# One more of eight u/gate pairs computed with seven block products: NF from 3 to 2 in a hybrid diffusion step

## The chip, the cores and the metric

The kernel runs on one core of a Trainium2 chip. The metric is the time of one execution on the device, in microseconds (us). Engines: PE multiplies matrices, DVE and ACT work element by element, POOL (GpSimd) does a few sums, SP issues the DMAs. Each engine works through its own list of instructions in order.

## The reference, cut to what matters

```
proj = jnp.matmul(h, p['w_in'])                  # h: 640 tokens x 2048
q, k, v, g_a, xbc, z, dt_raw, u, v_c, g_c, g_m = jnp.split(proj, _in_splits(), -1)
...
# branch C, the spatial gating unit
vs = jnp.einsum('gpq,bcqge->bcpge', p['w_s'], vn) + ...
y = u.astype(f32) * vs.reshape(b_, L, SGU_W) * jax.nn.silu(gate.astype(f32))   # gate is g_c
```

One input projection feeds three branches. Its columns are cut into tiles of 128 channels. Of u there are eight tiles, and eight of the gate g_c; u tile g and gate tile g are needed together with vs tile g. The 640 tokens are those of the prompt (128) and of the sample (512) together.

## The kernel before, in words

All large products are done in float32r with each operand split in two: hi is the value rounded to float32r, lo is what is left. A product is hi by hi, hi by lo, lo by hi: three matmuls.

**A plain tile** (`plain`, L207) multiplies one weight tile (16 blocks of 128 rows) with the 640 tokens in two halves of 320 columns: 16 x 3 x 2 = 96 matmuls of 320 columns. Its weights come in two DMAs (L125) of 1024 columns, ACT makes `whi` (L135) and DVE `wlo` (L136), 512 columns (four blocks) at a time.

**A pair** (`pair`, L219) computes two weight tiles at once. The two tiles, the two halves of the 2048 inner rows and the two halves of the tokens make a 2 by 2 block product, which is done with seven products instead of eight, by sums of blocks on both sides: 7 x 8 x 3 = 168 matmuls of 320 columns. The seven products are numbered 1 to 7. The weights' side is made in `fetch`: four DMAs (L184), the sums on POOL (L190, L191, L192, L198), then `parts`: ACT `whi` (L166) and DVE `wlo` (L167), in the order p1, p6, p7, p5, p4, p2, p3, two pieces of 512 columns each. The rings hold five raw weight buffers (`wraw`), four pieces of `whi` and of `wlo` (two products), and two sums (`s`).

The tokens' side of the pairs is made once, for k = 0 to 7: `make_t(k)` loads h again from DRAM (`ta`, `tb`, or `u`/`c` for the even k; L607 to L614), makes four differences on DVE (L617 to L620, 320 columns each) and splits three of them into `t12` (used by products 6 and 5) and `t4` (product 4) with `split_to` (ACT L597, DVE L598). The fourth difference, t3, later overwrites the second half of h_hi[k] and h_lo[k] (`make_t3`, names `hh` and `hl`), which a plain tile still reads; product 7 reads it. `ta` and `tb` of odd k have one buffer each, so a load for k + 2 waits until k is done.

The order of the program: after the normalisation stages one plain tile (NT_C), then the plain tiles of the first NF u/gate pairs, with the calls of `make_t` spread between them, then the `make_t3`, then the remaining u/gate pairs by seven products, then 51 more pairs of other columns, then the branches' projections with the attention between them, then the output projection.

```
    wseq = [("plain", NT_C)] + [("plain", n + g) for g in range(NF) for n in (NT_U, NT_GC)]
    wseq += [("pair", NT_U + g, NT_GC + g) for g in range(NF, 8)]
    ...
    fill = [(n + g, g) for g in range(NF) for n in (NT_U, NT_GC)]
    ...
        for k in range(i * 8 // len(fill), (i + 1) * 8 // len(fill)):
            make_t(k)
    for k in range(8):
        make_t3(k)
```

After each u/gate pair `post_c` (L550) multiplies: SiLU of the gate (ACT L546, DVE L547), u times vs (DVE L554), and the product of both on POOL (L555). The order on each engine is made by the scheduler of the language when the program is built, so a change of NF can move instructions that the source does not touch.

Of the kernel before, what the change touches and what calls it, by code (L numbers as in the profile page):

```python
# [19 lines left out]
EPS = 1e-6  # L20
NEG = -1.0e30
HALF = 320
NF = 3
MG = (6, 8, 10, 12)
SCRATCH = 1024

# [8 lines left out]
def hybrid_step(ctx: ExitStack, tc: tile.TileContext, a: dict, o: dict):  # L35
# [105 lines left out]

    wseq = [("plain", NT_C)] + [("plain", n + g) for g in range(NF) for n in (NT_U, NT_GC)]
    wseq += [("pair", NT_U + g, NT_GC + g) for g in range(NF, 8)]
    gates = [("pair", NT_GM + 16 * b + d, NT_GM + 16 * b + d + 1) for b in (2, 1, 0) for d in range(0, KD, 2)]
# [74 lines left out]
    def pair(job, B, tmp, out, seven=(1, 6, 7, 5, 4, 2, 3), side={}):  # L219

        ws = take(*job)
        ac = two_banks()
        bank = {1: ac[0], 5: ac[1], 6: sm_tile(), 7: sm_tile(), 4: sm_tile()}
        bank[2], bank[3] = bank[1], bank[5]
        t1, u2, u3 = (tmp(i) for i in range(3))
        c12, c21, c22 = out()
        done = set()
        for i in seven:  # L230
            ps = bank[i][:, :HALF]
            n = len(ws[i])
            for k, ((wh, wl), (bh, bl)) in enumerate(zip(ws[i], B[i])):
                TE.matmul(ps, wh, bh, start=(k == 0 and i not in (2, 3)), stop=False, skip_group_check=True)  # L234
                TE.matmul(ps, wh, bl, start=False, stop=False, skip_group_check=True)  # L235
                mm = TE.matmul(ps, wl, bh, start=False, stop=(k == n - 1), skip_group_check=True)  # L236
            done.add(i)
            at = None
            if i == 1:
                at = S.copy(t1, ps)  # L240
            if i == 6:
                at = V.tensor_tensor(u2, bank[6][:, :HALF], t1, op=ALU.add)
            if i in (6, 7) and {6, 7} <= done:
                at = V.tensor_tensor(u3, bank[7][:, :HALF], u2, op=ALU.add)
            if i in (7, 5) and {6, 7, 5} <= done:
                at = V.tensor_tensor(c22, bank[5][:, :HALF], u3, op=ALU.add)
            if i in (7, 4) and {6, 7, 4} <= done:
                at = V.tensor_tensor(c21, u3, bank[4][:, :HALF], op=ALU.subtract)
            if i == 3:
                at = V.tensor_tensor(c12, bank[5][:, :HALF], u2, op=ALU.add)  # L250
            for work in side.get(i, ()):
                work(mm, at)
        return [bank[1][:, :HALF], c12], [c21, c22]
# [265 lines left out]
    def post_conv(t, x):  # L519

        xq = pad[-1]
        S.copy(xq[:, 1:129], x[0][:, 0:128])
        S.copy(xq[:, 131:323], x[0][:, 128:320])
        S.copy(xq[:, 323:643], x[1])
        y = cvp.tile([P, 642], F32, tag="cvy", name="cvy")
        cw = cwh[:, 16 + 3 * t:16 + 3 * t + 3]
        V.tensor_scalar(y, xq[:, 1:643], cw[:, 1:2], cwh[:, t:t + 1], op0=ALU.mult, op1=ALU.add)
        V.scalar_tensor_tensor(out=y, in0=xq[:, 0:642], scalar=cw[:, 0:1], in1=y, op0=ALU.mult, op1=ALU.add)
        V.scalar_tensor_tensor(out=y, in0=xq[:, 2:644], scalar=cw[:, 2:3], in1=y, op0=ALU.mult, op1=ALU.add)
        r = gp.tile([P, 642], F32, tag="raw", name="cv")  # L530
        S.activation(r, y, AF.Tanh)
        V.scalar_tensor_tensor(out=r, in0=r, scalar=1.0, in1=y, op0=ALU.add, op1=ALU.mult)
        nc.sync.dma_start(out=cv_dram[:, t, :P], in_=r[:, :P])
        store(cv_dram[:, t, P:], r[:, 130:642])
# [15 lines left out]
    def post_c(g, u, gc):  # L550
        t = load_raw(g)
        for h in range(2):
            hs = (H1, H2)[h]
            V.tensor_tensor(t[:, hs], t[:, hs], u[h], op=ALU.mult)  # L554
        G.tensor_tensor(t, t, silu_of(gc), op=ALU.mult)  # L555
        nc.sync.dma_start(out=o_dram["c"][:, g, :], in_=t)
# [85 lines left out]
    post_conv(12, [b[:, :HALF] for b in ac])  # L642
    fill = [(n + g, g) for g in range(NF) for n in (NT_U, NT_GC)]
    u = None
# [25 lines left out]

    for g in range(NF, 8):
        x, y = pair(("pair", NT_U + g, NT_GC + g), HB, tmp_g, out_g,
                    (1, 2, 6, 5, 4, 7, 3) if g == NF else (1, 6, 7, 5, 4, 2, 3))
        post_c(g, x, y)
# [746 lines left out]
```

## Time and profile before

| what | value |
|---|---|
| median of 3 runs | 2521.35 us (2520.49 to 2522.02) |
| the profiled execution's own time | 2522.39 us |
| its span, first to last instruction | 2520.6 us |
| PE busy | 2429.2 us, 96% |
| DVE busy | 1735.2 us, 69% |
| ACT busy | 1084.2 us, 43% |
| POOL busy | 801.2 us, 32% |
| mean granted PE clock | 0.993 |

The span is what the profile's rows can explain; the 1.8 us around it are the start and the end of the execution. The shares are means over stages with different limits. The stretch that the change touches lies between about 270 and 400 us.

### The profile page before, as it was taken

What the parts mean: (1) busy time and instruction counts of PE and PEld (TensorE: products, weight loads), DVE (VectorE), ACT (ScalarE), POOL (GpSimd) and SP (SyncE); (2) the same over time, 40 slices, a digit from 0 to 9 for tenths busy, and PEclk for the clock granted to TensorE, in tenths of its full rate; (3) what the DMA queues carried; (4) which work ended last, traced back from release to release, by engine and by line L of the source; (5) the groups of instructions that cost most, each with busy time, mean ns of one, the idle gap of its engine ahead of it and who ended that gap; (6) DMA issues with size and microseconds to landing.
All of it is one profiled execution on the core that took longest, in us unless ns stands there. A gap on an engine that the chain in (4) does not pass through costs nothing. (4 is left out here: it accounts for less than half of the span.)

```text
span 2520.6 us, 43220 instructions
## 1 busy us (share of the span) xinstructions
PE 2429.2 (96%) x16615; PEld 2298.4 (91%) x16615; DVE 1735.2 (69%) x2788; ACT 1084.2 (43%) x2340; POOL 801.2 (32%) x369
## 2 busy tenths in 40 slices
PE   6989999999999999999999999999999999999998
PEld 4679999999999999999999999989998888998886
DVE  5454688888888778767677767777545555537975
ACT  4122233444444555565555554554323666322222
POOL 2100045444444344434333344344232233331001
PEclk9999999999999999999999999999999999999999
DMA  9953433333333444443444444434987554545544
GB/s 374 340 180 109 159 117 111 105 115 116 109 106 115 140 140 134 163 156 127 151 140 134 138 128 158 142 121 155 332 308 258 170 182 133 155 122 195 178 141 166
DMA packets 154072, 411.13 MB, mean 163 GB/s; under 512 B 16965, under 2 KB 29546, under 8 KB 153866
## 3 DMA queue, kind: packets, MB, share of 16 engines
q1 hardware_dynamic: 151562, 407.33, 48.4%
q8 instruction: 130, 2.13, 0.3%
q10 hardware_dynamic: 2304, 1.05, 0.1%
q14 instruction: 76, 0.62, 0.1%
HBM read 333.50 MB, written 74.81 MB: 162 GB/s over the span
## 5 line engine op out<-in xcount | busy, mean ns | idle before, releaser
L167 DVE TENSOR_TENSOR wlo<-wraw,whi 128x512 fp32r<-128x512 f32 x448 | 612.0, 1383 | 127.6 <-ACT whi L166 121.6
L166 ACT CAST whi<-wraw 128x512 fp32r<-128x512 f32 x448 | 275.1, 617 | 312.7 <-PE acca L235 147.4
L135 ACT CAST whi<-wraw 128x512 fp32r<-128x512 f32 (+1 forms) x238 | 140.3, 593 | 413.8 <-PE bk L824 140.5
L236 PE MATMUL acca<-hh,wlo 128*128 128x320 f32 x896 | 280.5, 313 | 15.0 <-DVE wlo L167 14.9
L166 ACT CAST whi<-s 128x512 fp32r<-128x512 f32 x336 | 203.0, 617 | 206.5 <-PE sm L235 82.5
L167 DVE TENSOR_TENSOR wlo<-s,whi 128x512 fp32r<-128x512 f32 x336 | 232.7, 693 | 73.6 <-ACT whi L166 69.5
L234 PE MATMUL acca<-hh,whi 128*128 128x320 f32 x896 | 278.5, 311 | 1.4 <-ACT whi L166 1.4
L235 PE MATMUL acca<-hl,whi 128*128 128x320 f32 x896 | 277.5, 310 | 0.0
L190 POOL TENSOR_TENSOR s<-wraw 128x1024 f32<-128x1024 f32 x56 | 145.7, 2602 | 369.3 <-DMA wraw<-in_w_nt 243.3
L136 DVE TENSOR_TENSOR wlo<-wraw,whi 128x512 fp32r<-128x512 f32 (+1 forms) x218 | 155.5, 716 | 143.7 <-ACT whi L135 143.0
L191 POOL TENSOR_TENSOR s<-s,wraw 128x1024 f32<-128x1024 f32 x56 | 150.3, 2684 | 261.0 <-DVE wlo L167 260.9
L198 POOL TENSOR_TENSOR s<-wraw,s 128x1024 f32<-128x1024 f32 x56 | 138.6, 2475 | 209.7 <-issue 189.5
L236 PEld LDWEIGHTS acca<-hh,wlo 128*128 128x128 f32 x896 | 168.7, 188 | 21.4 <-DVE wlo L167 21.1
L234 PEld LDWEIGHTS acca<-hh,whi 128*128 128x128 f32 x896 | 169.1, 189 | 2.0 <-ACT whi L166 2.0
L235 PEld LDWEIGHTS acca<-hl,whi 128*128 128x128 f32 x896 | 169.0, 189 | 0.0
L824 PE MATMUL bk<-oh,whi 128*128 128x320 f32 x512 | 163.6, 319 | 2.2 <-ACT oh L1014 1.5
L824 PE MATMUL bk<-ol,whi 128*128 128x320 f32 x512 | 158.5, 310 | 1.0 <-DVE ol L1015 0.5
L824 PE MATMUL bk<-oh,wlo 128*128 128x320 f32 x512 | 158.3, 309 | 0.0
L236 PE MATMUL sm<-t4h,wlo 128*128 128x320 f32 x448 | 142.5, 318 | 14.2 <-DVE wlo L167 14.2
L192 POOL TENSOR_TENSOR wraw<-wraw 128x1024 f32<-128x1024 f32 x56 | 152.1, 2715 | 4.3
L234 PE MATMUL sm<-t4h,whi 128*128 128x320 f32 x448 | 140.5, 314 | 1.9 <-ACT whi L166 1.9
L235 PE MATMUL sm<-t4l,whi 128*128 128x320 f32 x448 | 140.3, 313 | 0.0
(406 smaller groups left out, 6961.5 us busy)
## 6 DMA issues: line engine op xcount, KB each, us to landing
wraw<-in_w_nt SPq DMA_DIRECT2D x240, 512.0 KB, 3.8
wm<-in_w_ms SPq DMA_DIRECT2D x64, 512.0 KB, 7.4
wraw<-in_w_br SPq DMA_DIRECT2D x48, 512.0 KB, 4.8
wm<-in_w_mg SPq DMA_DIRECT2D x32, 512.0 KB, 3.9
wraw<-in_w_out SPq DMA_DIRECT2D x31, 512.0 KB, 3.9
g_gate<-sg SPq DMA_DIRECT2D x48, 320.0 KB, 2.6
gt<-g_gate SPq DMA_DIRECT2D x48, 320.0 KB, 4.4
ac_d<-Y SPq DMA_DIRECT2D x32, 256.0 KB, 3.1
```

The source lines that it names most:

```text
L135: S.copy(hi[:, :n], rv)
L136: eng.tensor_tensor(lo[:, :n], rv, hi[:, :n].bitcast(F32), op=ALU.subtract)
L166: S.copy(hi, src[:, i:i + 512])
L167: V.tensor_sub(lo, src[:, i:i + 512], hi.bitcast(F32))
L190: G.tensor_tensor(s1, a21, a22, op=ALU.add)
L191: G.tensor_tensor(s2, s1, a11, op=ALU.subtract)
L192: G.tensor_tensor(a21, a11, a21, op=ALU.subtract)
L198: G.tensor_tensor(s2, a12, s2, op=ALU.subtract)
L234: TE.matmul(ps, wh, bh, start=(k == 0 and i not in (2, 3)), stop=False, skip_group_check=True)
L235: TE.matmul(ps, wh, bl, start=False, stop=False, skip_group_check=True)
L236: mm = TE.matmul(ps, wl, bh, start=False, stop=(k == n - 1), skip_group_check=True)
L824: newest[0] = TE.matmul(*args, **kw)
```

## The change

One number changes: NF, the count of u/gate pairs whose two tiles are computed plainly.

```
-NF = 3
+NF = 2
```

Pair 2 (u tile 2 and gate tile 2) leaves the plain tiles and becomes the first of now six u/gate pairs by seven products. It takes the order (1, 2, 6, 5, 4, 7, 3) in the source that pair 3 had. The list `fill` has four plain tiles instead of six, so two `make_t` fall to each, where before it was one or two.

The built programs differ between the first plain tiles and the second pair, and again in some forty rows at the start of the attention, where branch B's operands are made (L1014, L1015); elsewhere the rows are the same.

On POOL, the three sums of the first pair's weights (s1, s2 and the difference in wraw) stand here before the change, behind both products of the first two gated tiles (L555):

```order
L555 TENSOR_TENSOR raw_2875<-raw_2875,sg_2879 128x640
L555 TENSOR_TENSOR raw_3167<-raw_3167,sg_3171 128x640
L190 TENSOR_TENSOR s1_3337<-wraw_3331,wraw_3333 128x1024
L191 TENSOR_TENSOR s2_3338<-s1_3337,wraw_3329 128x1024
L192 TENSOR_TENSOR wraw_3331<-wraw_3329,wraw_3331 128x1024
L198 TENSOR_TENSOR s2_3338<-wraw_3335,s2_3338 128x1024
```

and with the change:

```order
L555 TENSOR_TENSOR raw_2889<-raw_2889,sg_2893 128x640
L190 TENSOR_TENSOR s1_3090<-wraw_3084,wraw_3086 128x1024
L191 TENSOR_TENSOR s2_3091<-s1_3090,wraw_3082 128x1024
L192 TENSOR_TENSOR wraw_3084<-wraw_3082,wraw_3084 128x1024
L198 TENSOR_TENSOR s2_3091<-wraw_3088,s2_3091 128x1024
L555 TENSOR_TENSOR raw_3248<-raw_3248,sg_3252 128x640
L190 TENSOR_TENSOR s1_3316<-wraw_3310,wraw_3312 128x1024
L192 TENSOR_TENSOR wraw_3310<-wraw_3308,wraw_3310 128x1024
```

The first pair's sums moved ahead of the second L555, and the second pair's sums follow right behind it.

On DVE, from the first difference of k = 5 (L617, which needs the load `tb`) the rows before the change are these; `wlo` of L136 belongs to a plain tile:

```order
L617 TENSOR_TENSOR t3c_3184<-tb_3314,ta_3313 128x320
L618 TENSOR_TENSOR ta_3313<-ta_3313 128x320
L617 TENSOR_TENSOR t3d_3512<-c1_3509,ta_3506 128x320
L619 TENSOR_TENSOR tb_3314<-tb_3314,ta_3313 128x320
L136 TENSOR_TENSOR wlo_3068<-wraw_3061,whi_3067 128x512
L618 TENSOR_TENSOR ta_3506<-ta_3506 128x320
```

and with the change, down to the first weights of product 7 (`wlo_3112`):

```order
L617 TENSOR_TENSOR t3c_3055<-tb_3067,ta_3066 128x320
L167 TENSOR_TENSOR wlo_3108<-s2_3091,whi_3107 128x512
L547 SCALAR_TENSOR_TENSOR sg_3252<-sg_3252,acca_3080 128x320
L618 TENSOR_TENSOR ta_3066<-ta_3066 128x320
L547 SCALAR_TENSOR_TENSOR sg_3252<-sg_3252,accb_3081 128x320
L598 TENSOR_TENSOR t4l2_2458<-u0_3051,t4h2_2457 128x320
L598 TENSOR_TENSOR hl5_841<-t3c_3055,hh5_126 128x320
L617 TENSOR_TENSOR t3d_3265<-c1_3262,ta_3259 128x320
L167 TENSOR_TENSOR wlo_3112<-wraw_3084,whi_3111 128x512
```

Pieces of the first pair's weights (`wlo_3108` is the second half of product 6, `wlo_3112` the first half of product 7) and the `make_t3` splits (`hl5`) now stand among the differences.

On PE, the first pair comes to product 7 in this order with the change (`sm2` collects product 6, `sm3` product 7):

```order
L235 MATMUL sm2_3380<-t12l4_2446,whi_3107 128x320
L236 MATMUL sm2_3380<-t12h4_2445,wlo_3108 128x320
L234 MATMUL sm3_3381<-hh0_121,whi_3111 128x320
L235 MATMUL sm3_3381<-hl0_547,whi_3111 128x320
L236 MATMUL sm3_3381<-hh0_121,wlo_3112 128x320
```

The last of these is the 42nd matmul of that pair; before the change two more plain tiles stood in this place.

## Rows read from the trace of the kernel before

**Rows 1.** The page: PE's busy time, share of the span and instructions.
```profile
PE 2429.2 (96%) x16615; PEld 2298.4 (91%) x16615; DVE 1735.2 (69%) x2788; ACT 1084.2 (43%) x2340; POOL 801.2 (32%) x369
```

**Rows 2.** Windows: from:to, length, busy us (instructions) by engine, PE clock, DMA.
```profile
324.60:341.90 17.30, 15.18 (x98) 14.12 (x97) 16.04 (x27) 7.32 (x18) 4.30 (x2) 1.00 0.36 115
341.90:371.85 29.95, 28.58 (x194) 28.16 (x193) 23.93 (x28) 11.88 (x22) 13.87 (x6) 1.00 0.35 112
371.85:396.50 24.65, 24.65 (x171) 24.65 (x170) 20.93 (x26) 9.53 (x16) 12.34 (x6) 1.00 0.34 113
```

**Rows 3.** Timeline of PE: start, duration, instruction, [idle before <-releaser].
```profile
310.55 0.31 PE L217 MATMUL acca<-hh,whi 128*128 128x320 f32 x1
...
326.70 0.41 PE L217 MATMUL acca<-hh,wlo 128*128 128x320 f32 x1 [1.31 <-DVE wlo L136]
...
365.00 0.41 PE L236 MATMUL acca<-hh,wlo 128*128 128x320 f32 x1 [1.37 <-DVE wlo L167]
...
371.85 0.31 PE L234 MATMUL sm<-t12h,whi 128*128 128x320 f32 x1
```

**Rows 4.** Timeline of DVE, the same columns.
```profile
307.36 0.68 DVE L136 TENSOR_TENSOR wlo<-wraw,whi 128x512 fp32r<-128x512 f32 x1
307.96 0.48 DVE L598 TENSOR_TENSOR t12l<-tb,t12h 128x320 fp32r<-128x320 f32 x1
308.36 0.48 DVE L618 TENSOR_TENSOR ta<-ta 128x320 f32<-128x320 f32 x1
308.76 0.48 DVE L598 TENSOR_TENSOR t4l<-tb,t4h 128x320 fp32r<-128x320 f32 x1
...
314.61 0.49 DVE L617 TENSOR_TENSOR t3c<-tb,ta 128x320 f32<-128x320 f32 x1 [2.75 <-DMA tb<-h_d]
...
321.15 2.70 DVE L598 TENSOR_TENSOR t12l<-ta,t12h 128x320 fp32r<-128x320 f32 x1
...
375.57 0.49 DVE L242 TENSOR_TENSOR u<-sm,u 128x320 f32<-128x320 f32 x1 [0.56 <-PE sm L236]
```

**Rows 5.** Timeline of POOL, the same columns.
```profile
320.91 2.59 POOL L190 TENSOR_TENSOR s<-wraw 128x1024 f32<-128x1024 f32 x1 [0.84 <-DMA wraw<-in_w_nt]
...
326.05 2.85 POOL L192 TENSOR_TENSOR wraw<-wraw 128x1024 f32<-128x1024 f32 x1
343.98 2.42 POOL L198 TENSOR_TENSOR s<-wraw,s 128x1024 f32<-128x1024 f32 x1 [15.07 <-DVE wlo L167]
...
374.36 2.09 POOL L555 TENSOR_TENSOR raw<-raw,sg 128x640 f32<-128x640 f32 x1 [2.02 <-DVE raw L554]
```

**Rows 6.** Timeline of SP's DMA issues.
```profile
270.30 12.05 SPq L125 DMA_DIRECT2D wraw<-in_w_nt  x3
...
309.27 0.32 SPq L608 DMA_DIRECT2D tb<-h_d  x1
```

**Rows 7.** The page, DMA issues: count, KB each, us from issue to landing.
```profile
wraw<-in_w_nt SPq DMA_DIRECT2D x240, 512.0 KB, 3.8
```

**Rows 8.** Tile tb, 290 to 340 us (three loads).
```profile
DMA to landing us min/median/max: 2.9/4.9/5.2
```

**Rows 9.** Waits of PE, 1930 to 1980 us: total, times, longest.
```profile
PE sm L827 <- DVE mx L1039: 1.7, 1, 1.7
PE bk L824 <- ACT oh L1014: 1.5, 1, 1.5
```

**Rows 10.** Timeline of PE at 37 us.
```profile
37.23 0.50 PE L331 MATMUL v<-whi,hh 128*128 128x512 f32 x1 [2.49 <-ACT hh L359]
```

**Rows 11.** Windows of PE alone: from:to, length, busy (instructions), granted clock, DMA.
```profile
38.00:39.00 1.00, 1.00 (x4) 0.65 1.02 410
39.00:40.00 1.00, 1.00 (x4) 0.50 1.02 406
40.00:41.00 1.00, 1.00 (x4) 0.50 1.03 410
41.00:42.00 1.00, 1.00 (x4) 0.64 1.06 422
```

## The prediction

> **What bounds the kernel now.** I read the page first: PE is busy for 96% of the span [rows 1], so a change pays only by taking matmuls away or waits before them. The windows then show that the stretch around the change is not yet at that bound. The window 371.85:396.50 is one whole pair in its steady state: 24.65 us for 168 matmuls, with PE busy throughout, so 0.1467 us each [rows 2]. The two windows before it hold 2.1 and 1.4 us in which PE is idle outright, and more in which it only refills [rows 2].
>
> I take as the measuring stretch everything from the start of plain tile u2, at 310.55 us, to product 6 of pair 4, at 371.85 us [rows 3]: 61.30 us. It holds two plain tiles (192 matmuls), pair 3 (168) and product 1 of pair 4 (24), 384 in all: 384 x 0.1467 = 56.3 us. The other 5.0 us are waits. The timeline of PE shows the two largest: 1.31 us for the wlo of a plain tile and 1.37 us for the wlo of a pair [rows 3]. DVE was late because POOL was adding. L190 to L192 run from 320.91 to 328.90 us, and the DVE split that starts at 321.15 us takes 2.70 us in place of 0.48 us: it ends at 323.85 us, 0.34 us after L190's end at 323.51 [rows 4, 5]. A DVE instruction with one operand in PSUM keeps its 0.49 us while L555 runs [rows 4, 5]. So each POOL sum holds up one DVE instruction that reads only SBUF until the sum is over.
>
> **What the change takes away.** Pair 2 needs 168 matmuls instead of 192: 24 x 0.1467 = 3.5 us. The same stretch after the change holds 360 matmuls, 52.8 us, so without any wait it would end 8.5 us earlier: 3.5 us of matmuls and the 5.0 us of waits. The break-even is therefore 8.5 us of waits after the change, and the question is how many there will be.
>
> **What it adds beside PE.** ACT gets 6 more casts, DVE 6 more wlo at 0.60 us and five combinations at 0.40 us, their pitches in the timeline [rows 4], POOL four more sums of 2.4 to 2.9 us [rows 5]. In 25 us per pair these fit: the steady pair shows DVE busy 20.9 of 24.65 us, POOL 12.3 and ACT 9.5 with no wait [rows 2]. The four weight DMAs are those of the plain tiles, under another line. I cost these at nothing there. Around the first pair there is no such cover, because DVE must also make the operands.
>
> **The first pair's sums.** Its third weight block takes the place of the last of the three DMAs that run from 270.30 to 282.35 us, so it lands by about 282.0 + 3.8 = 285.8 us [rows 6, 7]. L190 to L192 then take 8.0 us [rows 5] and end near 293.8 us, before the differences begin. That removes the collision of 320.91 to 328.90 us.
>
> **The operands.** The plain tiles end at 310.55 instead of 341.9 us. The load of tb for k = 5 waits until the last split of k = 3 has freed the buffer. Before, that split starts at 308.76 and the load is issued at 309.27 us [rows 4, 6]. After the change two more DVE instructions (the splits of make_t3 and one difference that moved behind) stand ahead of it, 2 x 0.40 us, so the load is issued near 310.1 and lands, 4.9 to 5.2 us later [rows 8], near 315.2 us. Before, this wait (2.75 us, to 314.61 [rows 4]) hurt nobody, since the pair began 27 us later. Now the first pair is already running, and DVE's queue stands behind that load.
>
> **Wait A.** PE starts the pair at 310.55 and needs the first wlo of product 7 as its 42nd matmul: 310.55 + 41 x 0.1467 = 316.6 us. On DVE eight instructions from the late difference on stand ahead of that wlo: seven at 0.40 and one at 0.60, 3.4 us, then 0.68 for itself: 315.2 + 3.4 + 0.7 = 319.3 us. The wait is at least 2.7 us. But POOL's L198 can start as soon as product 6's wlo is done, at 316.3, and holds the next difference until 0.34 us past its end: 316.3 + 2.4 + 0.3 = 319.1 us. Then come SiLU, one split, and L555, which starts behind the SiLU near 319.5 us, runs 2.1 us and holds the split hl5 to 321.9 us. L617 and the wlo follow: 322.9 us. Wait A is 6.3 us by this, and I take it, since the trace has the same collision at full price.
>
> **Wait B.** From 322.9 us PE has 48 matmuls (7.0 us) to the first wlo of product 4, so it would be there at 329.9 us. Pair 3's third weight block can be fetched when product 7's second wlo is done, at 324.3; it lands near 328.3 us with 3.8 us of DMA [rows 7], and L190 and L192 run from 328.3 to about 333.6 us. They catch a t12 split of k = 6, which then ends at 331.1, and the wlo of product 4, which ends at 334.0 us. PE waits 1.4 and 2.7 us. The operands of k = 7 come last on DVE, each 0.4 us before its matmul; small waits of 1.3 us in all. Wait B is 5.4 us. Without a collision those for k = 7 come to 4.3 us instead, because tb of k = 7 is then what is late; that is its lower end.
>
> **The sum.** 6.3 + 5.4 = 11.7 us of waits against the 8.5 us of the break-even: +3.2 us. From pair 3 on the rows are the old ones. The lower bound is 2.7 + 4.3 = 7.0, that is -1.5 us. The upper one adds to both waits a load that is 1 us later, and a pair 3 that starts with its weights late: about +6. The profiled execution took 2522.39 us (span 2520.6), 1.0 above the median; the difference applies to both, and on the median of 2521.35 I forecast **2524.5 us**. The permuted rows at the attention's start I cost at nothing: the waits near them are 1.7 and 1.5 us [rows 9], so I allow 2 us on either side.
>
> **The rivals.** A measurement of this kernel tells a change from none at about 0.2%, 5.0 us.
>
> *Faster: the operands come in time.* If DVE catches up because neither L198, L555 nor the next L190 hits it and both tb loads land in 2.9 us as the fastest did [rows 8], the waits come to about 3 us and the time to 2516 us; with none, 2512.9. It decides if wait A and B together stay under 3.5 us. Against it stands the queue: even free of POOL the wlo is ready 2.7 us late.
>
> *No collision, but the late loads.* The lower bound above: 2519.9 us. It asks that POOL's sums fall between DVE's instructions. Against it: L198 is released by the very wlo that the next difference follows on DVE, so the two meet.
>
> *Slower by over 0.2%: PE's clock falls.* At 37 us, after 2.49 us idle, the granted clock goes to half, 1.2 GHz: four slices of 1 us show 0.65, 0.50, 0.50, 0.64 [rows 10, 11], a loss of 0.35 + 0.5 + 0.5 + 0.36 = 1.7 us. Wait A is longer than that idle time, and so a fall behind it is likely. It costs nothing as long as PE only comes later to wait B, which has 5.4 us to absorb 1.7. A second fall behind wait B has only the small waits of k = 7 to hide in. With one fall in the open +4.9, with both +6.6: 2526.2 to 2528 us. It decides where wait B ends later on PE's side than on DVE's.
>
> The Trainium skill, "TensorE: Matmul & The Clock Gate", Part 1, says that the throttled clock is the default and activity releases it, so a wait in mid-kernel is paid twice. By that rule both falls would be paid and the sum would be +6.6; by this case's rows the first hides in a wait that DVE sets, and the sum stays at +3.2. The trace agrees that idle time halves the clock (0.50 after 2.49 us), but shows no fall with DVE-bound work behind it.
>
> **Chances.** Forecast (waits of 10 to 13 us): 0.52, of which 0.08 lies beyond +5. No collision: 0.18. Faster: 0.07. Clock or a later stall that spreads to pair 3: 0.23, nearly all beyond +5. Hence faster 0.07, within 0.2% 0.63, slower 0.30. The range for 8 in 10 reaches from the lower bound less 1 us to two clock falls: 2518.9 to 2528.5 us.
>
> **What would show it.** In the profile after the change: 24 fewer matmuls; L190 to L192 of the first pair near 286 to 294 us; DVE idle for tb until about 315 us; a PE wait of about 6 us for wlo of L167 near 317 us and two more near 330; DVE instructions of 2 to 3 us under L198, L555, L190; product 6 of pair 4 near 374.5 instead of 371.85 us. The prediction is wrong if PE's waits between 310 and 345 us stay under 7 us, if the clock stays at half past 340 us, or if later pairs start to wait.

## The result and the profile after

The changed kernel takes 2536.44 us (median of 4 runs, 2533.68 to 2541.16) where the kernel before takes 2520.92 us on the same chip: a ratio of 1.0058, 95% interval [1.0043, 1.0073]. It is 15.5 us slower; the forecast was +3.2 us. The profiled execution took 2541.16 us (span 2539.4 us), 18.8 us over that of before.

The page of the changed kernel has the 24 matmuls less, and its instruction fetches are two rows of the DMA queues (packets, MB, share of 16 engines):

```profile
PE 2435.5 (96%) x16591; PEld 2301.5 (91%) x16591; DVE 1741.0 (69%) x2799; ACT 1088.7 (43%) x2347; POOL 811.9 (32%) x373
...
q8 instruction: 130, 2.13, 0.4%
...
q14 instruction: 77, 0.63, 0.1%
```

The timeline of PE around the first pair, to be held against [rows 3]:

```profile
317.14 0.41 PE L236 MATMUL sm<-t12h,wlo 128*128 128x320 f32 x1 [1.88 <-DVE wlo L167]
...
323.53 0.63 PE L236 MATMUL sm<-hh,wlo 128*128 128x320 f32 x1 [5.07 <-DVE wlo L167]
323.96 0.47 PE L234 MATMUL sm<-hh,whi 128*128 128x320 f32 x1
324.23 0.47 PE L235 MATMUL sm<-hl,whi 128*128 128x320 f32 x1
...
336.30 0.42 PE L234 MATMUL sm<-hh,whi 128*128 128x320 f32 x1 [1.76 <-ACT hh L597]
...
376.99 0.31 PE L234 MATMUL sm<-t12h,whi 128*128 128x320 f32 x1
```

The first pair starts at 309.53 us here, and product 6 of pair 4 at 376.99: 67.46 us, against 61.30 us in the same stretch of before. Here the change costs 6.2 us. Of the 67.46 us, 52.8 are matmuls at full clock and 8.7 are the three waits; the other 6.0 us are the clock and the refilling behind waits. Behind the wait of 5.07 us the matmuls follow each other by 0.27 us in place of 0.1467 us: TensorE runs at the lower of its two levels, 1.2 GHz. The clock had fallen before that wait, behind the first one of 1.88 us: in windows of 1 us it is 0.77 from 317 us, 0.50 in each window from 318 to 327, and 1.00 from 328 us. It falls again behind the wait of 1.76 us: 0.51, 0.50 and 0.50 from 338 to 341 us. The windows of the changed kernel (PE, PEld, DVE, ACT, POOL, granted clock, DMA) show the same in steps of 10 us:

```profile
310.00:320.00 10.00, 6.58 (x39) 5.69 (x38) 7.65 (x14) 4.17 (x11) 2.36 (x1) 0.88 0.52 174
320.00:330.00 10.00, 6.47 (x31) 6.47 (x32) 9.70 (x19) 4.60 (x10) 1.91 (x2) 0.61 0.41 126
330.00:340.00 10.00, 7.95 (x43) 6.57 (x42) 8.89 (x12) 4.22 (x9) 4.93 (x2) 0.90 0.16 60
340.00:350.00 10.00, 10.00 (x65) 10.00 (x65) 9.10 (x16) 4.47 (x8) 2.69 (x1) 0.93 0.33 110
350.00:360.00 10.00, 10.00 (x71) 10.00 (x70) 8.41 (x10) 3.99 (x7) 4.53 (x2) 1.00 0.42 128
```

The timelines of DVE and POOL show the load of tb and the collisions, as [rows 4, 5] did for before:

```profile
316.00 0.49 DVE L617 TENSOR_TENSOR t3c<-tb,ta 128x320 f32<-128x320 f32 x1 [2.35 <-DMA tb<-h_d]
...
317.40 2.52 DVE L618 TENSOR_TENSOR ta<-ta 128x320 f32<-128x320 f32 x1
...
320.65 1.82 DVE L598 TENSOR_TENSOR hl<-t3c,hh 128x320 fp32r<-128x320 f32 x1
```

```profile
285.97 2.40 POOL L190 TENSOR_TENSOR s<-wraw 128x1024 f32<-128x1024 f32 x1 [2.58 <-DMA wraw<-in_w_nt]
...
317.22 2.36 POOL L198 TENSOR_TENSOR s<-wraw,s 128x1024 f32<-128x1024 f32 x1 [23.56 <-DVE wlo L167]
320.40 1.72 POOL L555 TENSOR_TENSOR raw<-raw,sg 128x640 f32<-128x640 f32 x1 [0.82 <-DVE sg L547]
```

So far this is close to what the prediction drew. But the stretch explains only 6.2 of the 15.5 us. Laid over each other pair by pair (start of product 1 to start of the next), the two traces agree within 0.01 us from pair 5 to 640 us, 24.64 to 25.73 us each; then the changed kernel loses at some pairs and gains at others (the pair at 1253 us in before takes 28.28 us there, 25.08 us after). The largest loss in a pair is at the one that starts at 871.5 us in before: 24.64 us there, 28.85 us after. These are its start and the next one's, first before, then after:

```profile
871.49 0.31 PE L234 MATMUL acca<-hh,whi 128*128 128x320 f32 x1
...
896.13 0.31 PE L234 MATMUL acca<-hh,whi 128*128 128x320 f32 x1
```

```profile
876.98 0.31 PE L234 MATMUL acca<-hh,whi 128*128 128x320 f32 x1
...
905.83 0.31 PE L234 MATMUL acca<-hh,whi 128*128 128x320 f32 x1
```

The chain behind the loss is short. xk_d, ac_d and cv_d are scratch tensors in DRAM through which another branch passes its data while the pairs run. In the timelines of SP, ACT and PE of the changed kernel, two stores go out at 884.28 and 884.75 us; the load behind them (L689) reuses the first one's buffer and is issued only when that store has landed; ACT's casts stand behind its data, and PE behind a cast:

```profile
884.28 0.43 SPq L775 DMA_DIRECT2D xk_d<-ssq  x1
...
884.75 0.49 SPq L776 DMA_DIRECT2D ac_d<-Y  x1
...
891.24 0.32 SPq L689 DMA_DIRECT2D ssq<-acum_d  x1
...
895.24 0.63 ACT L725 ACTIVATE Y<-ssq 128x512 f32<-128x512 f32 x1 [7.03 <-DMA ssq<-acum_d]
...
896.72 0.41 PE L234 MATMUL acca<-hh,whi 128*128 128x320 f32 x1 [1.98 <-ACT whi L166]
```

Of the 4.2 us, 2.0 are this wait; behind it the granted clock is 0.50 in the three windows from 898 to 901 us. In before the load follows the first store by 4.8 us instead of 7.0 (timeline of SP):

```profile
878.69 0.43 SPq L775 DMA_DIRECT2D xk_d<-ssq  x1
879.46 0.32 SPq L776 DMA_DIRECT2D ac_d<-Y  x1
883.49 0.32 SPq L689 DMA_DIRECT2D ssq<-acum_d  x1
```

What the DMA engines did meanwhile is in the view of DMA (GB/s in 40 slices of the window, queues, issues with KB and us to landing). First the changed kernel from 884 to 892 us, then before from 878 to 886 us:

```profile
GB/s 143 61 143 369 287 246 184 143 197 236 361 274 335 353 407 384 381 402 369 443 325 318 223 228 177 82 13 26 26 26 26 26 26 33 20 31 10 0 0 0
...
q8 instruction: 1, 0.02, 0.7%
...
xk_d<-ssq SPq DMA_DIRECT2D x1, 320.0 KB, 6.9
...
ac_d<-Y SPq DMA_DIRECT2D x1, 256.0 KB, 7.0
```

```profile
GB/s 0 0 143 102 184 328 348 164 184 225 182 195 233 297 317 364 369 397 420 415 382 402 384 348 274 225 215 133 21 0 0 0 154 205 269 218 205 179 192 141
...
xk_d<-ssq SPq DMA_DIRECT2D x1, 320.0 KB, 4.7
...
ac_d<-Y SPq DMA_DIRECT2D x1, 256.0 KB, 4.6
```

After the change there is a packet of q8 in the window, 0.7% of 16 engines over 8 us, that is 0.9 us of one engine; and the stores end in a tail of 2 us at 26 GB/s, a sixteenth of what all engines moved before it. In before this window has no q8 packet and no tail.

By its count q8 carries TensorE's instructions: 130 packets for 2.13 MB are 16.4 KB each, and 2 x 16591 matmuls and weight loads over 130 packets are 255 instructions, or 128 matmuls. At 0.1467 us a matmul that is one packet every 18.8 us; between 390 and 880 us each trace has 26, one every 18.8 us. The place of a packet goes with the count of matmuls: in each of the 16 profiles of this document the packets between 420 and 1700 us start, in the median, when TensorE stands at the 64th to 66th matmul of a block of 128, counted from the start of the program. The change takes away 24 matmuls, so that from pair 3 on every packet comes 24 matmuls, or 3.5 us, later in the program.

### The profile page after: what moved, and what is told of

The parts are those of the page before. It is cut to its first block, busy times and chain, and to the rows that moved or that the text cites. A ratio compares the mean times of both kernels' runs of the same rounds, so it can differ in the third digit from the quotient of the medians.

```text
span 2539.4 us, 43203 instructions
## 1 busy us (share of the span) xinstructions
PE 2435.5 (96%) x16591; PEld 2301.5 (91%) x16591; DVE 1741.0 (69%) x2799; ACT 1088.7 (43%) x2347; POOL 811.9 (32%) x373
## 3 DMA queue, kind: packets, MB, share of 16 engines
q8 instruction: 130, 2.13, 0.4%
## 5 line engine op out<-in xcount | busy, mean ns | idle before, releaser
L167 DVE TENSOR_TENSOR wlo<-wraw,whi 128x512 fp32r<-128x512 f32 x456 | 620.9, 1379 | 130.9 <-ACT whi L166 120.7
L236 PE MATMUL acca<-hh,wlo 128*128 128x320 f32 x912 | 286.1, 314 | 14.9 <-DVE wlo L167 14.9
L234 PE MATMUL acca<-hh,whi 128*128 128x320 f32 x912 | 284.7, 312 | 3.8 <-ACT whi L166 3.8
L235 PE MATMUL acca<-hl,whi 128*128 128x320 f32 x912 | 283.3, 311 | 0.0
L190 POOL TENSOR_TENSOR s<-wraw 128x1024 f32<-128x1024 f32 x57 | 148.1, 2598 | 385.2 <-DMA wraw<-in_w_nt 245.4
L136 DVE TENSOR_TENSOR wlo<-wraw,whi 128x512 fp32r<-128x512 f32 (+1 forms) x210 | 151.5, 724 | 143.7 <-ACT whi L135 143.0
L198 POOL TENSOR_TENSOR s<-wraw,s 128x1024 f32<-128x1024 f32 x57 | 141.3, 2478 | 218.1 <-issue 184.8
L192 POOL TENSOR_TENSOR wraw<-wraw 128x1024 f32<-128x1024 f32 x57 | 154.3, 2707 | 4.4
L236 PE MATMUL sm<-hh,wlo 128*128 128x320 f32 x456 | 141.8, 311 | 5.1 <-DVE wlo L167 5.1
L234 PE MATMUL sm<-hh,whi 128*128 128x320 f32 x456 | 142.0, 311 | 1.8 <-ACT hh L597 1.8
```

Of the source, the lines that this page charges most:

```text
L136: eng.tensor_tensor(lo[:, :n], rv, hi[:, :n].bitcast(F32), op=ALU.subtract)
L167: V.tensor_sub(lo, src[:, i:i + 512], hi.bitcast(F32))
L190: G.tensor_tensor(s1, a21, a22, op=ALU.add)
L192: G.tensor_tensor(a21, a11, a21, op=ALU.subtract)
L198: G.tensor_tensor(s2, a12, s2, op=ALU.subtract)
```

## The experiments

Their expectations weigh these theories. For the time behind the first pair: **stall** (the first pair's waits and the clock bring the later losses along), **order** (the permuted rows at the attention's start do), **shift** (any displacement does), **chance** (single late transfers, different in every execution), **fetch** (TensorE's instruction packets now meet other transfers). For the first pair itself: **collision** (each hold by a POOL sum is paid by TensorE) and **queue** (DVE has that much work ahead, and a hold only moves it).

The kernel before has a median of 2516.9 to 2519.3 us on the chips of these runs, and single runs from 2511.8 to 2524.8; each difference below is to the median of before on the same chip. "Stretch" is the time from the start of the first pair (before: of tile u2) to product 2 of pair 4, read in each profile: 75.38 us before (310.55 to 385.93), 81.54 us after (309.53 to 391.07), so +6.2. "Rest" is the difference of the medians less that of the stretch. The stretch is read in one execution of each kernel. Where two kernels have the same instructions in it, it is the same to 0.3 us (before twice, the changed kernel twice), or differs by 1.2 us (the changed kernel and after_start24) and 1.6 us (nocoll and nocoll_start24), so that smaller steps are not told apart.

**after_again**: no edit. 

> The changed kernel once more, unedited. Its profile showed +5.1 us up to pair 5 and further losses at scattered places (880, 1430, 1680, 1790, 1940, 2180 us), 18.8 us in all. If these places belong to the program (stall theory or order theory), the new profile shows losses at the same places and the same sum within 3 us. If they are chance landings of single transfers (shift theory: after a disturbance each execution falls differently), the local +5 us stays and the other places change, with the total anywhere between 2531 and 2542 us.

Measured: 2534.79 us, +17.9, ratio 1.0067 [1.0052, 1.0082]; stretch +6.1, rest +11.8. The pair at 871 us takes 28.24 us and the xk_d store 6.1 us. The loss belongs to the program.

**before_again**: no edit. 

> The kernel before once more, unedited, for a second profile of it. Chance theory (the places of the later losses are single late transfers, different in every execution): its pairs take other times at other places than in the first profile, as much as the changed kernel's do. Fetch theory (the 16 KB fetches of TensorE's instructions, one every 18.9 us, stand at fixed places in the program and delay the transfers that they meet): the fetches stand where they stood, the stores of cv_d at 650 us land in 3.1 to 3.5 us again, and the sum behind pair 5 is within 3 us of the first profile's.

Measured: 2519.07 us in its only run. The pair at 871 us takes 24.78 us, the xk_d store 4.7 us, the cv_d stores at 650 us 3.3 and 3.5 us; the sum behind pair 4 is within 1.2 us of the first profile's. Chance has its part: one pair near 1572 us takes 30.88 us here and 24.98 us in the first profile, and the first profile's 28.28 us at 1253 us is 26.99 here. But these come in both directions.

**shift_28** and **shift_40**: the kernel before with 28 or 40 more matmuls in a plain tile (the edit for 28):

```diff
-            for w, x, first, last in ((wh, h_hi, k == 0, False), (wh, h_lo, False, False),
+            for w, x, first, last in ((wh, h_hi, True, True),) * (14 * (n == NT_GC + 2 and k == 0)) + ((wh, h_hi, k == 0, False), (wh, h_lo, False, False),
```

> The kernel before with 28 more matmuls in the gate's plain tile of pair 2 (28 x 0.1467 = 4.1 us, no wait; every other engine keeps its order everywhere). Stall theory and order theory: before + 4.1 us = 2525 us, the later stages as in before. Shift theory (everything behind is sensitive to any displacement): before + 4.1 + 8 to 13 us = 2533 to 2538 us.

> The kernel before with 40 more matmuls at the same place (40 x 0.1467 = 5.9 us, no wait); at this count the rows at the attention's start stand in the order of the changed kernel, so it is the permuted order without the new pair. Stall theory: before + 5.9 = 2527 us. Order theory: before + 5.9 + some 5 us at the attention's start and behind = 2531 to 2533 us, with the losses past 1930 us only. Shift theory: 2535 to 2540 us with losses from 880 us on.

Measured: 2523.76 us, +6.9, ratio 1.0031 [1.0017, 1.0045], and 2522.26 us, +5.4, ratio 1.0022 [1.0012, 1.0032]. The stretch grew by only 0.8 and 2.5 us, where 4.1 and 5.9 us were expected, because the matmuls fill waits that TensorE had there: of the idle 3.5 us of before, 1.4 are left in either kernel. So a rest of 6.1 and 2.9 us is left. shift_40 has nearly the changed kernel's order at the attention's start (8 of ACT's rows and 2 of DVE's stand otherwise) and the smaller rest of the two: the order theory falls. So does shift as such, since the larger displacement costs less.

**e2_bufs**: the changed kernel with other tiles for the operands of k = 3 and 5 (t4[3] and t12[7], whose space they take, are made at k = 6 and 7):

```diff
-            sa, sb = slot(15, F32, "ta"), slot(14, F32, "tb")
+            sa, sb = [tslot(22 - 4 * k + 12 + i, F32, n) for i, n in enumerate(("ta", "tb"))] if k in (3, 5) else (slot(15, F32, "ta"), slot(14, F32, "tb"))
```

> The changed kernel with tiles of their own for the operands of k = 3 and k = 5 (in the space of the operands that are made last), so that no load waits for the last split of the odd k before it. All theories: the load for k = 5 lands before 312 us, product 6's second wait (1.88 us) goes and wait A falls from 5.1 to 1 to 3 us; locally 4 to 6 us are won. Stall theory: the later losses go too, total 2513 to 2522 us. Order or shift theory: the later losses stay, total 2529 to 2533 us.

Measured: 2533.37 us, +16.5, ratio 1.0061 [1.0046, 1.0076]; stretch +4.4, rest +12.0. The stretch is 1.7 us shorter, not 4 to 6: its waits are 4.05, 0.84, 1.43 and 1.76 us, and DVE is now busy without a gap from 304 to 327 us.

**ph_after24**, **ph_after64**, **ph_before104**: small matmuls ahead of the pair g = 3 set TensorE's count (24, 64 or 104):

```diff
-        t1, u2, u3 = (tmp(i) for i in range(3))
+        t1, u2, u3 = (tmp(i) for i in range(3)); [TE.matmul(bank[6][:, :2], ws[6][0][0], B[6][0][0][:, :2], start=True, stop=True, skip_group_check=True) for _ in range(24 * (job[1] == NT_U + 3))]
```

> The changed kernel with 24 more matmuls of 2 columns ahead of its second pair (g = 3): work of at most 1 to 2 us, and every instruction of TensorE behind it stands at the same count as in the kernel before, so its instruction fetches meet the program where they did there. Fetch theory: the later losses go back to those of before, 8 to 10 us less than the changed kernel, 2524 to 2528 us where that has 2535; the cv_d stores near 655 us land in 3.1 to 3.5 us in place of 4.6 to 5.3. Chance theory or stall theory: 0 to 2 us more than the changed kernel, 2535 to 2538 us.

> The kernel before with 104 more matmuls of 2 columns ahead of the pair g = 3. A fetch brings the instructions of 128 matmuls, so 104 more is 24 fewer: the fetches meet the program where they do in the changed kernel, without its first pair. Fetch theory: before + the small matmuls' own time (read from the trace, 3 to 6 us) + 8 to 10 us, so 2528 to 2535 us on a base of 2517; the cv_d stores near 655 us land in 4.6 to 5.3 us. Chance or stall theory: before + the small matmuls' own time alone, 2520 to 2523 us.

> The changed kernel with 64 more matmuls of 2 columns at the same place: half a fetch away from its own count, 40 matmuls away from before's. Fetch theory: the later losses are neither kernel's; the cv_d stores near 655 us land in 3.1 to 3.5 us unless a fetch stands there, and the time is the changed kernel's + 2 to 4 us of small matmuls - 0 to 10 us. Chance or stall theory: the changed kernel's + 2 to 4 us, 2537 to 2541 us.

Measured for ph_after24, ph_before104 and ph_after64, in the order of their expectations: 2528.08 us, +9.1, ratio 1.0034 [1.0021, 1.0046]; 2549.3 us, +30.4, ratio 1.012 [1.0102, 1.0137]; 2536.92 us, +18.0, ratio 1.007 [1.0057, 1.0082]. The small matmuls were priced wrongly. 24 of them take 2.73 us, but 64 take 10.02 us and 104 take 18.81 us, because the clock falls among them. In the windows of ph_after64 (PE alone) TensorE is busy with nothing else, and the granted clock goes to half:

```profile
347.96 10.02 PE L227 MATMUL sm<-t12h,whi 128*128 128x2 f32 x64
```

```profile
350.00:351.00 1.00, 1.00 (x12) 1.00 0.00 0
351.00:352.00 1.00, 1.00 (x11) 0.97 0.00 0
352.00:353.00 1.00, 1.00 (x7) 0.50 0.12 44
353.00:354.00 1.00, 1.00 (x7) 0.50 0.74 284
```

They follow each other by 0.112 us at full clock and by 0.213 us at half. All this stands in the stretch: +10.5, +21.0, +17.2 us. The rest is -1.4 us at before's count, +9.3 us where the kernel before is given the changed one's, +0.7 us at the third. The cv_d stores took 3.8 and 4.0 us (a little above what was expected), 4.4 and 4.5 (a little below), 3.5 and 3.6 us. In these three kernels some rows of SP near the pair and some tens of rows at the attention's start stand in another order too, so the count is not the only difference; in the next two it nearly is.

**after_start24** and **before_start24**: the same 24 at the very start, where TensorE has nothing to do:

```diff
-    xp = st.enter_context(tc.tile_pool(name="xp", bufs=3))
+    xp = st.enter_context(tc.tile_pool(name="xp", bufs=3)); z = xp.tile([P, P], F32R, tag="z", name="z", bufs=1); V.memset(z.bitcast(F32), 0.0); zp = ps_tile("m"); [TE.matmul(zp[:, :2], z, z[:, :2], start=True, stop=True) for _ in range(24)]
```

> The changed kernel with 24 matmuls of 2 columns on a tile of zeros at the very start, in the first 11 us in which TensorE is idle; no other instruction changes its place on any engine. TensorE's instructions from pair 3 on then stand at the count that they have in the kernel before. Fetch theory: the later losses go without costing anything, so before + 5 to 7 us (the local waits and the clock alone), 10 to 12 us less than the changed kernel. Stall or chance theory: the changed kernel's time, before + 15 to 18 us.

> The kernel before with the same 24 matmuls at the start; no other instruction changes its place. Its count then stands 24 matmuls on the other side of before's than the changed kernel's does, near that of the 28 matmuls of shift_28. Fetch theory: the pair at 871 us takes 25.8 to 26.3 us in place of 24.64 (as with 28 and 40 more), the fetches stand 3.5 us earlier in the program, and the sum behind pair 5 moves by up to 3 us either way. Stall or chance theory: the time of before within 1 us. What it tells above all is whether 24 matmuls at the start do anything by themselves.

Measured: 2526.93 us, +7.7, ratio 1.0036 [1.0021, 1.005], and 2525.56 us, +6.3, ratio 1.0023 [1.001, 1.0036]. The same edit makes the changed kernel 8 to 10 us faster, against the +15.5 and +17.9 us without it on other chips, and the kernel before 6 us slower; beside one memset on DVE it adds and moves no other instruction. In the profile of after_start24 the 24 matmuls lie in the idle time (timeline of PE), and the two stores at 888 us land early (view of DMA, 888 to 896 us):

```profile
1.09 5.28 PE L287 MATMUL m<-z 128*128 128x2 f32 x24 [1.09 <-DVE z L287]
11.19 1.11 PE L315 MATMUL v<-cm,x 128*128 128x128 f32 x4 [4.83 <-DVE x L312]
```

```profile
xk_d<-ssq SPq DMA_DIRECT2D x1, 320.0 KB, 2.8
...
ac_d<-Y SPq DMA_DIRECT2D x1, 256.0 KB, 3.1
```

Its stretch in the profiled execution is +7.3, its rest by the medians +0.3 us. That execution was the slowest of its eight, 2536.79 us against the median of 2526.93, and itself takes 7.2 us more than before behind the stretch, at other places; so for this kernel the rest stands on the medians alone. For before_start24 I had expected a move of at most 3 us; the rest is +6.4. Its pair at 871 us takes 26.03 us, as expected.

**nocoll**, **nocoll_start24**: e2_bufs with two POOL sums on DVE, without and with the 24 matmuls at the start:

```diff
-            G.tensor_tensor(s2, a12, s2, op=ALU.subtract)
+            (V if len(fetched) == 2 * NF + 1 else G).tensor_tensor(s2, a12, s2, op=ALU.subtract)
...
-        G.tensor_tensor(t, t, silu_of(gc), op=ALU.mult)
+        (V if g == 1 else G).tensor_tensor(t, t, silu_of(gc), op=ALU.mult)
```

> The changed kernel with tiles of their own for k = 3 and 5 (as in e2_bufs), and the two sums of GpSimd that held DVE there (L198 of the first pair, L555 of pair 1) made on DVE. Collision theory (each sum's hold, 2.0 and 1.5 us in e2_bufs, is paid in full by TensorE): locally 2 to 3.5 us less than e2_bufs, +1 to +2 in place of +4.2 us, in all 2529 to 2531 where e2_bufs has 2533. Queue theory (DVE has that much work in front of the pair, and a hold only moves it): within 1 us of e2_bufs.

> The same with the 24 matmuls at the start. Fetch theory and collision theory together: before + 1 to 3 us. Fetch theory and queue theory: before + 4 to 6. Stall or chance theory: as nocoll, before + 12 to 16.

Measured: 2530.0 us, +10.7, ratio 1.0046 [1.003, 1.0061], stretch +2.8, rest +8.0; and 2522.44 us, +3.2, ratio 1.001 [1.0001, 1.002], stretch +1.2, rest +2.0. These two kernels were measured on one chip and differ by the 24 matmuls and the memset alone: 7.6 us. What the two holds were worth in the stretch is known only roughly: it goes from e2_bufs' +4.4 to +2.8 in nocoll and to +1.2 in nocoll_start24, which has the same instructions there. The two have nearly the same waits (6.9 and 6.4 us) but not the same clock, 0.76 and 0.88 on the mean from 326 to 340 us.

The same stores in these two, nocoll from 879 to 887 us and nocoll_start24 from 878 to 886 us (view of DMA; the second has no q8 row):

```profile
q8 instruction: 1, 0.02, 0.7%
...
xk_d<-ssq SPq DMA_DIRECT2D x1, 320.0 KB, 6.6
```

```profile
xk_d<-ssq SPq DMA_DIRECT2D x1, 320.0 KB, 4.6
```

**nocoll2_start24**, **own_dve_start24**: the last two holds as well, or tiles of their own for k = 2 to 5:

```diff
-            G.tensor_tensor(s1, a21, a22, op=ALU.add)
-            G.tensor_tensor(s2, s1, a11, op=ALU.subtract)
-            G.tensor_tensor(a21, a11, a21, op=ALU.subtract)
+            E = V if len(fetched) == 2 * NF + 2 else G
+            E.tensor_tensor(s1, a21, a22, op=ALU.add); G.tensor_tensor(s2, s1, a11, op=ALU.subtract)
+            E.tensor_tensor(a21, a11, a21, op=ALU.subtract)
...
+        own = {2: 14, 3: 22, 4: 12, 5: 22}.get(k)
...
+            sa, sb = (tslot(own, F32, "ta"), tslot(own + 1, F32, "tb")) if own else (slot(15, F32, "ta"), slot(14, F32, "tb"))
```

> nocoll_start24 with the two sums of GpSimd that still hold DVE's operands of k = 7 there (L190 and L192 of pair 3, holds of 1.9 and 2.2 us at 324 to 329 us) made on DVE too, 1.2 us each. Collision theory: the last two waits of TensorE (1.16 and 2.46 us, for hh and hl of k = 7) lose 1.5 to 2 us together, and the clock's fall behind them goes: 2 to 4 us less than nocoll_start24, that is before - 1 to + 1. Queue theory: the waits stay, within 1 us of nocoll_start24, before + 2 to 4.

> nocoll_start24 with tiles of their own for the operands of k = 2, 3, 4 and 5, so that no load but that of k = 6 waits for a split; the order on DVE becomes another one, with k = 7 finished before product 4's last operands. If the late loads still set the end: 2 us less than nocoll_start24. If DVE's queue does (43 of its 64 instructions for the operands stand behind the first pair's first wlo in every variant): within 1.5 us of nocoll_start24.

Measured: 2521.86 us, +2.7, ratio 1.0009 [0.9999, 1.0018], stretch +1.5; and 2520.53 us, +1.4, ratio 1.0009 [0.9997, 1.0021], stretch +0.7. The stretch stays within 0.5 us of nocoll_start24's +1.2, where the collision theory wanted 2 to 4 us less: it falls for these last two holds. What is left of the stretch is put down to DVE's queue; no run shortened that. No variant beats the kernel before.

All runs by TensorE's count behind pair 3 against before's (104 more is 24 fewer, since a packet holds 128):

| count | kernels | stretch, us | rest, us |
|---|---|---|---|
| 0 | after_start24, ph_after24, nocoll_start24, nocoll2_start24, own_dve_start24 | +7.3, +10.5, +1.2, +1.5, +0.7 | +0.3, -1.4, +2.0, +1.3, +0.7 |
| -24 | the changed kernel, after_again, e2_bufs, nocoll, ph_before104 | +6.2, +6.1, +4.4, +2.8, +21.0 | +9.4, +11.8, +12.0, +8.0, +9.3 |
| +24, +28 | before_start24, shift_28 | -0.1, +0.8 | +6.4, +6.1 |
| +40 | shift_40, ph_after64 | +2.5, +17.2 | +2.9, +0.7 |

In these runs the rest goes with the count, whatever the operands, the waits of the first pair and the number of plain tiles are. It is known to some 3 to 4 us, by the intervals of the ratios. The profiles alone say the same without the medians: from product 2 of pair 4 to the last instruction the seven at before's count (before, before_again and the first row) take 2129.9 to 2141.9 us, on the mean 2134.9, and the five at -24 take 2139.3 to 2148.3, on the mean 2143.7. That is 8.8 us. The four others take 2135.4 to 2140.3; there the loss is smaller and less sure, only 1.2 us more than before in shift_28.

That a packet delays the store which it meets can be read across the 16 profiles, since the packets stand elsewhere in kernels of other counts. The xk_d store near 880 us lands in 6.1 to 6.9 us in the five profiles at -24, where a q8 packet starts while it runs or just as it is issued, and in 2.8 to 4.9 us in the eleven others, where none does. Of the places behind 400 us at which a store meets a packet in some profiles and none in others, 92 can be compared: the store lands 0.96 us later with the packet on the mean, and later at 76 of them. Which losses follow depends on the place, and no count is good everywhere: the pair at 1253 us takes 26.1 to 28.4 us in the seven profiles at before's count and 25.1 to 25.3 in the nine others.

## Why the prediction was wrong

**What bounds, and the matmuls**: right. 24 matmuls went, and 0.1467 us each still holds in the steady pairs.

**The first pair's sums and the load of tb**: right. L190 starts at 285.97 us, predicted 286; tb is used from 316.00 us, predicted 315.2.

**Wait A**: right in size, with one row more. Predicted 6.3 us for product 7's first wlo, by L198 and L555; measured 5.07 us there and 1.88 us for product 6's last wlo, 6.95 in all. Both sums held DVE as drawn: L198's 2.36 us stretched the difference to 2.52 us, L555's 1.72 us the split to 1.82 us. Taking both holds and the late loads away moved the stretch by 3.4 us (+6.2 to +2.8), and by 6.1 us where both kernels have the 24 matmuls at the start (+7.3 to +1.2), so collisions and late loads, with the clock that goes with them, are half or more of what the change costs there; the rest is put down to DVE's queue, which no run shortened.

The Trainium skill, "SBUF — State Buffer", "SBUF: two separate sides", says that DVE and GpSimd share a pair of ports which one instruction holds to its end. The trace agrees: 2.52 us in place of 0.48 us under a sum of 2.36 us.

**Wait B**: oversized. Predicted 5.4 us, measured 1.76 us, for k = 7 alone. L190 and L192 did hold two DVE instructions (329.81 to 335.01 us). The first hold cost next to nothing: the wlo of product 4 was ready at 332.76 us, and TensorE, forecast there at 329.9 us, began the matmul in front of it only at 332.43, late by its waits and its clock. The second (the split t4l, 2.67 us, to 335.35 us) stands directly in front of the difference and the cast for which TensorE waits until 336.30 us.

**The clock**: undersized. I priced a fall at 1.7 us and let the first one hide in wait B. It came earlier, inside wait A, behind the 1.88 us, and lasted past 327 us. The granted clock is 0.88, 0.61, 0.90 and 0.93 in the four windows from 310 us on, and waits, clock and refilling share one sum: 8.7 + 6.0 = 14.7 us in place of 11.7 + 0. So the stretch came out at +6.2 for +3.2 us: mechanism right, size off, and this alone would have been inside the range. (The 374.5 us that I gave for product 6 of pair 4 does not follow from the sum either: 310.55 + 52.8 + 11.7 is 375.05; it came at 376.99.)

**"From pair 3 on the rows are the old ones"**: this step failed, and with it the forecast. Behind pair 3 the rows are the old ones, up to the attention's start in the old order, and they take 9.4 us longer where the prediction put nothing. I counted what the 24 matmuls cost and not what their absence moves: the packets in which TensorE's instructions arrive. Where a packet falls into a store that a later load waits for, the store can end 2 us later; the first such place, the cv_d stores near 650 us, shows 3.1 and 3.4 us before and 5.1 and 5.3 us after. That the count decides is shown, by restoring it at no cost (rest +0.3 us; 7.6 us between nocoll and nocoll_start24) and by giving it to the kernel before (+9.3 us). That it acts through the packet on the DMA engines is read from the profiles, where packet, tail and late landing go together; no run moved a packet without the count, and the 9.4 us were not followed place by place. DVE and ACT also have more instructions than before (11 and 7 in the page), and their packets (q14) moved too; since restoring TensorE's count was enough, their part is taken to be small.

The Trainium skill, "Runtime: NRT & Kernel Launch", "Instruction fetch mechanics", says that instructions are refilled in blocks of 16 KiB, or 256 instructions, and that crossing a block is mostly hidden. The size agrees with this trace (16.4 KB, 255 instructions). That it is hidden holds for TensorE itself, whose steady pairs of 24.64 us hold such packets without a wait, but not for the transfers that the block meets: the xk_d store takes 6.9 us in place of 4.7.

**The permuted rows at the attention's start**, costed at nothing: not contradicted. shift_40 has nearly the same order and a rest of 2.9 us, which its other count may explain; and after_start24, which has the order itself, has a rest of +0.3 us.

## What to carry to other kernels

In a kernel that is tight everywhere, a change that alters the number of instructions of the busiest engine moves all of that engine's instruction fetches behind it against the other transfers; here 24 matmuls fewer cost 8 to 12 us behind the place of the change, and 24 or 28 more about 6 us by the medians. Before judging such a change, restore the count with idle instructions where the engine waits anyway (its first 11 us here) and compare at equal counts; at equal count this change is +7.7 us, and with tiles of their own for its operands and two sums moved to DVE +1.4 us, which is no gain. And a wait in the middle of a full engine is paid again in its clock and in refilling: 6.0 us on 8.7 us of waits.

## What the hardware showed that I had not expected

- Where one 16 KB instruction packet (0.9 us of one DMA engine) meets a 320 KB store, the store takes 6.9 us in place of 4.7, and the delay reaches TensorE through a buffer that is written again.
- A matmul of 2 columns with its own weight load takes 0.112 us at full clock, not much less than one of 320 columns (0.1467 us), and 0.213 us at half. In a row of 64 or 104 of them the granted clock fell to 0.50 while TensorE was busy throughout; the 24 at the very start follow each other by 0.213 us too.
- 28 more matmuls in front of the pair (4.1 us) cost the kernel before only 0.8 us there: they fill part of the waits that the prediction had counted as 5.0 us (idle outright: 3.5 us before, 1.4 with them).
- The same kernel spreads over 10 us from run to run on some chips (before: 2511.83 to 2522.21 in 18 runs) and over 1.5 us in the four runs on the first one.
